# Two more seven-product pairs in a transformer block's down projection, a later place for one pair of residual products, and a later half of the token sums

## The chip, the cores and the metric

The kernel runs on one core of one Trainium2 chip. The time of a kernel is the device time of one execution in microseconds (us), and its figure is the median of several executions. A profile is one further execution, recorded by the hardware profiler: it has a span (from the first to the last recorded work) and a device time of its own, which is a little longer than the span.

Five engines matter. PE (TensorE) multiplies matrices; PEld is its loading of the stationary operand, which overlaps the multiplying. DVE (VectorE) and ACT (ScalarE) work elementwise, POOL (GpSimd) does a few tiny things here, and SP (SyncE) issues the transfers from memory.

## The reference, cut to what matters

One layer of a hybrid encoder with 256 tokens and 2048 features: an input projection, retention and latent attention side by side, an output projection with a normalised residual, and then a feed-forward part:

```
x = LN(alpha * x + concat(A, B) @ W_out)
x = LN(alpha * x + relu(x @ W_up)^2 @ W_down)
```

`W_up` is 2048 x 8192 and `W_down` is 8192 x 2048, all in float32. The change touches only the last product, `relu(...)^2 @ W_down`, and the residual sum behind it.

## The kernel before

**Splitting.** Every float32 operand of a large product is split into a high part `hi` in the narrower format fp32r and the rest, `lo = value - hi`. A product is then three matmuls: `hi*hi`, `hi*lo` and `lo*hi`. ACT makes each `hi` (line 381 for the down projection) and DVE each `lo` (line 382). So each weight that comes from memory passes ACT and DVE once before PE can use it.

**The down projection.** The 8192 rows of `W_down` are 64 blocks of 128, taken two at a time as 32 *pairs*, and the 2048 output columns are two halves, passes `p = 0` and `p = 1`. The tokens are two blocks of 128. In a pass, an ordinary pair takes 24 matmuls of 128x512: 2 row blocks, 2 token blocks, 2 column quarters, 3 split terms (`xstat`, line 297). They accumulate in four PSUM banks `cb`. The `relu^2` values are held in `rr` and split, four row blocks at a time, by `r_split` (lines 969 and 970).

**Seven-product pairs.** A pair is a 2x2 block product (two token blocks, two row blocks, two column quarters), so it can be done with seven block products in place of eight, as in Strassen-Winograd's scheme. Such a pair takes 21 matmuls (line 1062, `seven_products`). For it, DVE and ACT make sums of the tokens (`token_sums`, lines 389 to 395) and sums of the weights (`weight_sums`, lines 401 to 404), and the weights are split in four pieces (three of 1024 columns and one of 512) where an ordinary pair has two of 1024. `SEVEN` (line 38) lists, for each pass, which pairs in order of use are done so: seven in the first, six in the second. The four sums `mb` of such pairs are added to the residual when the last of a pass is done, by `add_sums`.

**Order of the work.** The program order of each engine is written out by hand. The work that prepares weights is a list of jobs, each a list of pieces, and a job's transfer is issued when one of three buffers `raw` comes free (`load_ahead`). The main loop calls `unit()` after each group of matmuls (four times in a pair of either kind). `unit()` first takes each generator in `side` one step further, and then emits up to two pieces, as long as one of the five slots for split weights (`NSLOT`, tile names `hi_wd` and `lo_wd`) is free in program order. In an ordinary pair one `unit()` call stands behind every 6 matmuls.

**The last residual.** In the second pass `add_sums` does one thing more: the residual's last quarter for the second token block, `col(1, 3)`, isn't added by DVE at the end. It is split into `xb` (lines 1035 and 1036) and added into PE's bank `cb[1][1]` by two matmuls with an identity (`identr`, line 1032; the matmuls are line 1040). These matmuls stand 6 steps of the generator, and so 6 `unit()` calls, behind the split. The last four pairs of the second pass (`w_staged`) are kept for the end, where they are used bank by bank so that the normalisation can begin on the first banks.

Of the kernel before, what the change touches and what calls it, by code (L numbers as in the profile page):

```python
# [8 lines left out]
F32 = mybir.dt.float32  # L9
# [25 lines left out]


ORDER = (tuple(range(16)), (14, 15, 11, 12, 13) + tuple(range(11)))
SEVEN = ((2, 6, 10, 14, 18, 22, 26), (2, 6, 10, 14, 18, 22))
KEPT = {11: 0, 12: 1, 13: 2}
NHELD = 4  # L40
STAGE_AT = 24
# [34 lines left out]
def kernel(  # L76
# [19 lines left out]
    nc = tc.nc  # L96
# [60 lines left out]
    def raw_tile(job, name):  # L157
        job.raw = wraw.tile([P, 2048], F32, tag="raw", name=name)
        return job.raw
# [182 lines left out]
    def row_job(i, pieces):  # L342
        def load(job):
            norm_rows[i] = raw_tile(job, f"row{i}")
            nc.sync.dma_start(norm_rows[i], ln_rows[i:i + 1].partition_broadcast(P))
        other(load, pieces)
# [17 lines left out]
    def weights_pair(p, pair, into=None, seven=None):  # L364
        job = Job(None, [], into is None or None in into)

        def load():
            raw = raw_tile(job, f"raw_wd{p}_{pair}")
            nc.sync.dma_start(raw.rearrange("p (e c) -> p e c", e=2),
                              w_down[2 * pair:2 * pair + 2, :, p * 1024:(p + 1) * 1024].rearrange("e p c -> p e c"))  # L370

        def split(i, src, n=1024):
            if into is None or into[i] is None:
                hi = wsp.tile([P, 1024], F32R, tag="hi", name=f"hi_wd{p}_{pair}_{i}")
                lo = wsp.tile([P, 1024], F32R, tag="lo", name=f"lo_wd{p}_{pair}_{i}")
            else:
                o = into[i] * 2048
                hi, lo = extra["sx"][:, o:o + 1024], extra["sx"][:, o + 1024:o + 2048]
            job.hi.append(hi)
            job.lo.append(lo)  # L380
            nc.scalar.copy(hi[:, 0:n], src)  # L381
            nc.vector.tensor_sub(lo[:, 0:n], src, hi[:, 0:n].bitcast(F32))  # L382

        def token_sums():

            k = 2 * pair
            r0, r1 = (rr[k // 32][:, k % 32 + e] for e in range(2))
            st = spare_flat[:, seven * 512:(seven + 1) * 512].rearrange("p (i c) -> p i c", i=4)
            nc.vector.tensor_add(st[:, 0], r0[:, P:], r1[:, P:])
            nc.vector.tensor_sub(st[:, 1], st[:, 0], r0[:, 0:P])  # L390
            nc.vector.tensor_sub(st[:, 2], r0[:, 0:P], r0[:, P:])
            nc.vector.tensor_sub(st[:, 3], r1[:, 0:P], st[:, 1])
            v = sums_of(seven)
            nc.scalar.copy(v[:, :, 0], st)
            nc.vector.tensor_sub(v[:, :, 1], st, v[:, :, 0].bitcast(F32))

        def weight_sums():

            b11, b12, b21, b22 = (job.raw[:, i * 512:(i + 1) * 512] for i in range(4))
            t1, t3, t4 = extra["t13"][:, 0:512], extra["t13"][:, 512:], extra["t4"]  # L400
            nc.vector.tensor_sub(t1, b12, b11)
            nc.vector.tensor_sub(t3, b22, b12)
            nc.vector.tensor_sub(b12, b22, t1)
            nc.vector.tensor_sub(t4, b21, b12)

        job.load = load
        if seven is None:
            job.pieces = [lambda e=e: split(e, job.raw[:, e * 1024:(e + 1) * 1024]) for e in range(2)]
            job.loose = 0 if into is None else 2 - into.count(None)
        else:  # L410
            job.loose = 2
            job.pieces = [token_sums, weight_sums, lambda: split(0, job.raw[:, 1024:]),
                          lambda: split(1, job.raw[:, 0:1024]), lambda: split(2, extra["t13"]),
                          lambda: split(3, extra["t4"], 512)]
        job.free = [[False] for _ in job.pieces[job.loose:]]
        jobs.append(job)
        return job

    def sums_of(q):
        return extra["sx"][:, q * 1024:(q + 1) * 1024].rearrange("p (i h c) -> p i h c", i=4, h=2)  # L420
# [3 lines left out]
    for p in range(2):  # L424
        for n, pair in enumerate(pairs[p]):
            if p == 0 or n < 32 - NHELD:
                j_down[p][pair] = weights_pair(p, pair, None, SEVEN[p].index(n) % 2 if n in SEVEN[p] else None)
                if p == 1 and n == STAGE_AT:
                    pair = pairs[1][32 - NHELD]
                    j_down[1][pair] = weights_pair(1, pair, (2, 3))  # L430
            elif n > 32 - NHELD:
                j_down[p][pair] = weights_pair(p, pair, (1, None) if n == 33 - NHELD else None)
    j_down[0][pairs[0][SEVEN[0][0]]].held = True
    row_job(2, [])
# [528 lines left out]
    def r_split(b, keep=None):  # L963
        if keep is None:
            t = work.tile([P, 4, 512], F32R, tag="big", name="rhl", bufs=2)
        else:
            t = extra["sx"][:, (keep + 1) * 2048:(keep + 2) * 2048].rearrange("p (k t) -> p k t", k=4)
        r = rr[b // 8][:, b % 8 * 4:b % 8 * 4 + 4]
        nc.scalar.copy(t[:, :, 0:S], r)
        nc.vector.tensor_sub(t[:, :, S:], r, t[:, :, 0:S].bitcast(F32))  # L970
        rhls[b] = t
# [28 lines left out]
    extra["t4"] = ut  # L1000
    j_down[0][pairs[0][SEVEN[0][0]]].held = False
    st2 = [stat.tile([P, 4, 6], F32, tag=f"ln{tb}", name=f"lm{tb}", bufs=1) for tb in range(2)]
    u, v = spare_flat[:, 0:512], spare_flat[:, 512:]

    def col(tb, j):
        return xt[:, tb, j * 512:(j + 1) * 512]

    def add_sums(p, mb):

        p1, p6, p5, p7 = mb  # L1010

        def plus(j, tb, src):
            c = col(tb, 2 * p + j)
            nc.vector.scalar_tensor_tensor(c, c, ALPHA, src, op0=ALU.mult, op1=ALU.add)

        nc.scalar.copy(u, p1)
        plus(0, 0, p1)
        yield
        nc.vector.tensor_add(u, u, p6)
        nc.vector.tensor_add(v, u, p7)  # L1020
        yield
        plus(0, 1, v)
        nc.vector.tensor_add(v, v, p5)
        yield
        plus(1, 1, v)
        nc.vector.tensor_add(u, u, p5)
        yield
        plus(1, 0, u)
        if p == 1:

            c = col(1, 3)
            nc.vector.tensor_copy(identr, ident)
            nc.scalar.activation(mask, ident, AF.Copy, scale=-1.0)
            xb = work.tile([P, 2, 512], F32R, tag="xf", name="xb")
            nc.scalar.copy(xb[:, 0], c)
            nc.vector.tensor_sub(xb[:, 1], c, xb[:, 0].bitcast(F32))
            for _ in range(6):
                yield
            for i in range(2):
                nc.tensor.matmul(cb[1][1], identr, xb[:, i], start=False, stop=False)  # L1040
# [7 lines left out]
    def seven_products(p, pair, first, last):  # L1048
        job = j_down[p][pair]
        x, k, q = rhls[pair // 2], pair % 2 * 2, SEVEN[p].index(pairs[p].index(pair)) % 2  # L1050
        for a, w, o, pb, alone in ((("x", 1, 0), 0, 0, cb[0][0], False), (("s", 3), 0, 512, cb[0][1], False),
                                   (("x", 0, 0), 1, 0, mb[0], True), (("s", 1), 1, 512, mb[1], True),
                                   (("s", 0), 2, 0, mb[2], True), (("s", 2), 2, 512, mb[3], True),
                                   (("x", 1, 1), 3, 0, cb[1][0], False)):
            use(job, w + 1)
            if a[0] == "x":
                h, l = (x[:, k + a[1], i * S + a[2] * P:i * S + (a[2] + 1) * P] for i in range(2))
            else:
                h, l = (sums_of(q)[:, a[1], i] for i in range(2))
            hi, lo = job.hi[w][:, o:o + 512], job.lo[w][:, o:o + 512]  # L1060
            for x_part, w_part, fst, lst in ((h, hi, True, False), (h, lo, False, False), (l, hi, False, True)):
                nc.tensor.matmul(pb, x_part, w_part, start=alone and first and fst, stop=alone and last and lst)  # L1062
            if o or w == 3:
                free(job, (w,))
                unit()

    for p in range(2):
        cb = [[(acc, bank)[p](f"d{p}{tb}{j}") for j in range(2)] for tb in range(2)]
        mb = None
        for n, pair in enumerate(pairs[p][:32 if p == 0 else 32 - NHELD]):  # L1070
            b = pair // 2
            if n % 2 == 0:
# [5 lines left out]
                if p == 1 and n == STAGE_AT:  # L1078
                    r_split(ORDER[1][15], -1)
            if n in SEVEN[p]:  # L1080
                if mb is None:
                    mb = [(bank, acc)[p](f"s{p}{j}") for j in range(4)]
                seven_products(p, pair, n == SEVEN[p][0], n == SEVEN[p][-1])
                if n == SEVEN[p][-1]:
                    side.append(add_sums(p, mb))
            else:
                job = j_down[p][pair]
# [152 lines left out]
```

## Time and profile before

| what | value |
|---|---|
| median of 3 runs | 1128.78 us (1127.2 to 1128.94) |
| the profiled execution | 1127.41 us, of which the span is 1125.4 us |
| PE busy | 1115.1 us, 99% of the span |
| DVE busy | 784.4 us, 70% |
| ACT busy | 548.4 us, 49% |
| DMA | 217.14 MB, mean 193 GB/s |
| granted TensorE clock | full (1.00) |
| down projection on PE | from about 773.2 us to 1116.3 us of the span |

A row of the timeline or of the chain of waits has a start in the span, a duration, an engine, a line of the kernel and the tiles that it writes and reads. A row "x4" merges four instructions of one kind; its duration runs from the start of the first to the end of the last. Square brackets give the idle time of the engine in front of the row, and what ended it.

### The profile page before, as it was taken

How to read it: one execution, taken by the hardware profiler on the slowest of the kernel's cores; microseconds unless marked ns; L12 is line 12 of the kernel's file. 1: busy time of each engine (PE TensorE's matmuls, PEld its weight loads, DVE VectorE, ACT ScalarE, POOL GpSimd, SP SyncE). 2: the span in 40 equal slices, each digit the busy share in tenths (PEclk: the TensorE clock that was granted, in tenths of full speed). 3: DMA queues.
4: the chain of work that ended last, by engine and by line, in shares of the span. 5: the costliest groups of instructions: out<-in, count | busy, mean ns of one | idle time of the engine just before them, and what ended most of it. 6: DMA issues, size and time to landing. Idle time of an engine off the chain costs nothing.

```text
span 1125.4 us, 14360 instructions
## 1 busy us (share of the span) xinstructions
PE 1115.1 (99%) x5609; PEld 948.4 (84%) x5609; DVE 784.4 (70%) x1089; ACT 548.4 (49%) x709; POOL 9.6 (1%) x18
## 2 busy tenths in 40 slices
PE   9999999999999999999999999999999999999988
PEld 8888888888888889888888888888888888888875
DVE  6676774656656786555555576657887887887885
ACT  4445564545453555444444444444555554555550
POOL 0000000000000000000000000000000000000000
PEclk9999999999999999999999999999999999999999
DMA  8755374444474635555555565654655555655562
GB/s 292 239 206 178 119 247 158 159 150 164 150 286 173 243 126 190 189 188 191 192 192 191 192 229 190 227 187 151 209 202 187 206 205 186 216 196 187 202 247 75
DMA packets 42387, 217.14 MB, mean 193 GB/s; under 512 B 4176, under 2 KB 5200, under 8 KB 27088
## 3 DMA queue, kind: packets, MB, share of 16 engines
q1 hardware_dynamic: 42176, 215.97, 54.5%
q8 instruction: 44, 0.72, 0.3%
q10 hardware_dynamic: 144, 0.26, 0.1%
q14 instruction: 23, 0.19, 0.0%
HBM read 214.12 MB, written 2.10 MB: 192 GB/s over the span
## 4 chain that ended last, share of the span: by engine, by line
PE 97%; DVE 1%; DMA 1%; issue 0%; ACT 0%; POOL 0%; POOLq 0%; SPq 0%; DVEq 0%
PE d L297 24%; PE up L682 20%; PE r L297 16%; PE up L688 10%; PE o L297 8%; PE m L297 4%; PE s L1062 3%; PE d L1062 2%; PE pu L682 2%; PE pv L297 1%; DMA raw_mla<-in_w_mla 1%; PE pu L688 1%; PE pq L297 1%; PE up L853 1%; PE pms L713 0%; PE pms L712 0%
## 5 line engine op out<-in xcount | busy, mean ns | idle before, releaser
L682 PE MATMUL up<-x1hl,hi_wu 128*128 128x512 f32 x984 | 234.8, 391 | 0.0
L682 PEld LDWEIGHTS up<-x1hl,hi_wu 128*128 128x128 f32 x984 | 180.8, 188 | 35.0
L382 DVE TENSOR_TENSOR lo_wd<-raw_wd,hi_wd 128x1024 fp32r<-128x1024 f32 x125 | 148.9, 1219 | 45.2 <-ACT hi_wd L381 44.6
L186 DVE TENSOR_TENSOR lo_wu<-raw_wu,hi_wu 128x1024 fp32r<-128x1024 f32 x128 | 155.8, 1224 | 22.8 <-ACT hi_wu L185 18.5
L381 ACT CAST hi_wd<-raw_wd 128x1024 fp32r<-128x1024 f32 x125 | 128.9, 1051 | 86.7 <-PE d L297 63.0
L297 PE MATMUL d<-hi_wd,rhl 128*128 128x512 f32 x616 | 167.7, 389 | 0.0
L185 ACT CAST hi_wu<-raw_wu 128x1024 fp32r<-128x1024 f32 x128 | 134.0, 1055 | 30.8 <-PE up L682 26.1
L297 PE MATMUL r<-hi_ret,xhl 128*128 128x512 f32 x512 | 147.1, 397 | 0.0
L297 PEld LDWEIGHTS d<-hi_wd,rhl 128*128 128x128 f32 x616 | 115.6, 188 | 24.0
L688 PEld LDWEIGHTS up<-x1hl,lo_wu 128*128 128x128 f32 x984 | 126.2, 191 | 4.7
L688 PE MATMUL up<-x1hl,lo_wu 128*128 128x256 f32 x984 | 127.7, 283 | 0.0
L297 PEld LDWEIGHTS r<-hi_ret,xhl 128*128 128x128 f32 x512 | 93.9, 188 | 18.2
L957 ACT COPY ut<-up 128x256 f32<-128x256 f32 x64 | 23.8, 372 | 170.0 <-PE up L682 167.4
L958 DVE TENSOR_TENSOR ut<-ut,up 128x256 f32<-128x256 f32 x64 | 26.9, 420 | 106.0 <-ACT ut L957 105.7
L297 PE MATMUL d<-lo_wd,rhl 128*128 128x512 f32 x308 | 95.1, 389 | 0.0
L186 DVE TENSOR_TENSOR lo_ret<-raw_ret,hi_ret 128x1024 fp32r<-128x1024 f32 x64 | 75.7, 1220 | 23.9 <-ACT hi_ret L185 23.7
L297 PE MATMUL r<-lo_ret,xhl 128*128 128x512 f32 x256 | 79.4, 391 | 0.0
L185 ACT CAST hi_ret<-raw_ret 128x1024 fp32r<-128x1024 f32 x64 | 64.9, 1051 | 16.4 <-PE r L297 12.2
L297 PEld LDWEIGHTS d<-lo_wd,rhl 128*128 128x128 f32 x308 | 57.8, 188 | 12.0
L297 PE MATMUL o<-hi_wo,mix 128*128 128x512 f32 x208 | 57.1, 392 | 0.0
L297 PEld LDWEIGHTS r<-lo_ret,xhl 128*128 128x128 f32 x256 | 48.0, 188 | 10.4
L297 PE MATMUL d<-hi_wd,sx 128*128 128x512 f32 x176 | 49.5, 389 | 0.0
(243 smaller groups left out, 1381.3 us busy)
## 6 DMA issues: line engine op xcount, KB each, us to landing
raw_wu<-in_w_up SPq DMA_DIRECT2D x64, 1024.0 KB, 4.8
raw_wd<-in_w_down SPq DMA_DIRECT2D x64, 1024.0 KB, 5.5
raw_ret<-in_w_ret SPq DMA_DIRECT2D x32, 1024.0 KB, 4.8
raw_wo<-in_w_out SPq DMA_DIRECT2D x16, 1024.0 KB, 4.8
raw_mla<-in_w_mla SPq DMA_DIRECT2D x14, 672.0 KB, 5.3
raw_qk<-in_w_qk SPq DMA_DIRECT2D x8, 640.0 KB, 3.9
row<-in_ln_rows SPq DMA_DIRECT2D x4, 1024.0 KB, 5.6
raw_uv<-in_w_uv SPq DMA_DIRECT2D x2, 1024.0 KB, 5.0
```

Of the source, the lines that this page charges most:

```text
L185: nc.scalar.copy(hi[:, o:e], r)
L186: nc.vector.tensor_sub(lo[:, o:e], r, hi[:, o:e].bitcast(F32))
L297: nc.tensor.matmul(accs[j][:, :w], x_part, w_part[:, a:a + w], start=first and fst and i == 0, stop=last and lst and i == len(steps) - 1)
L381: nc.scalar.copy(hi[:, 0:n], src)
L382: nc.vector.tensor_sub(lo[:, 0:n], src, hi[:, 0:n].bitcast(F32))
L682: nc.tensor.matmul(pb, hi[:, a:a + P], hl[:, k0 + i], start=first and i == ks[0], stop=last and i == ks[-1])
L688: nc.tensor.matmul(pb[:, 0:S], lo[:, a:a + P], hl[:, k0 + i, 0:S], start=False, stop=last and i == ks[-1])
L853: nc.tensor.matmul(pb[:, :, t], hi[:, k * P:(k + 1) * P], x1hl[:, k].rearrange("p (a t) -> p a t", a=2)[:, :, t], start=tb == 0 and k == 0 ...
L957: nc.scalar.copy(t, pb[:, S:])
L958: nc.vector.tensor_add(t, t, pb[:, 0:S])
L1062: nc.tensor.matmul(pb, x_part, w_part, start=alone and first and fst, stop=alone and last and lst)
```

## The change

Three edits. The list of seven-product pairs has eight pairs in the first pass and seven in the second (fifteen in all, thirteen before); they stand three or four pairs apart, where they stood four apart. The last DVE instruction of `token_sums`, which makes the low parts of the token sums out of what ACT has just written, is emitted behind the four weight sums in place of ahead of them. And the two matmuls that add the last residual are emitted 12 steps behind its split in place of 6.

```diff
-SEVEN = ((2, 6, 10, 14, 18, 22, 26), (2, 6, 10, 14, 18, 22))
+SEVEN = ((2, 5, 9, 12, 16, 19, 23, 26), (2, 6, 9, 13, 16, 19, 22))
...
             v = sums_of(seven)
             nc.scalar.copy(v[:, :, 0], st)
-            nc.vector.tensor_sub(v[:, :, 1], st, v[:, :, 0].bitcast(F32))
+            job.rest = lambda: nc.vector.tensor_sub(v[:, :, 1], st, v[:, :, 0].bitcast(F32))
...
             nc.vector.tensor_sub(b12, b22, t1)
             nc.vector.tensor_sub(t4, b21, b12)
+            job.rest()
...
             nc.scalar.copy(xb[:, 0], c)
             nc.vector.tensor_sub(xb[:, 1], c, xb[:, 0].bitcast(F32))
-            for _ in range(6):
+            for _ in range(12):
                 yield
             for i in range(2):
                 nc.tensor.matmul(cb[1][1], identr, xb[:, i], start=False, stop=False)
```

## The prediction

> **What bounds the kernel now.** First the page: the span and the busy times.
>
> ```profile
> span 1125.4 us, 14360 instructions
> ...
> PE 1115.1 (99%) x5609; PEld 948.4 (84%) x5609; DVE 784.4 (70%) x1089; ACT 548.4 (49%) x709; POOL 9.6 (1%) x18
> ```
>
> PE is the bound. An edit helps if it takes matmuls away or closes a hole in PE; more work on DVE or ACT costs nothing until it comes late for PE. Next I read what PE and its loads waited for from 770 us to the end, the stretch that the diff touches.
>
> ```profile
> PE d L1040 <- DVE identr L1032: 2.8, 1, 2.8
> PE sh L1154 <- ACT warm L1152: 1.4, 1, 1.4
> ...
> PEld d L1040 <- ACT sx L381: 3.2, 1, 3.2
> ```
>
> Ahead of the final normalisation (L1154) there is one hole in the whole down projection: at the two residual products, L1040. The chain in order of time gives the price of a matmul (four pieces of a regular cycle):
>
> ```profile
> 805.12 1.36 PE d L1062 x6
> 806.48 2.72 PE s L1062 x12
> 809.20 0.68 PE d L1062 x3
> 809.88 16.32 PE d L297 x72
> ```
>
> 72 matmuls in 16.32 us are 0.2267 us each. An ordinary pair (24) takes 5.44 us, a seven-product pair (21) 1.36 + 2.72 + 0.68 = 4.76 us. Four pairs with one of seven take 21.08 us.
>
> **Part 1: two more seven-product pairs.** Each turns 24 matmuls into 21: 3 x 0.2267 = 0.68 us, so 1.36 us for both. That is the whole direct gain; the rest of this part asks whether DVE can pay. Busy time of each engine in one such cycle; the others are alike. Columns: stretch, its length, then PE, PEld, DVE, ACT:
>
> ```profile
> 795.04:816.12 21.08, 21.08 (x95) 17.45 (x94) 17.45 (x21) 12.22 (x14) 0.00 (x0) 1.00 0.57 203
> ```
>
> DVE is busy 17.45 of 21.08 us. What leaves a cycle when it shrinks from four pairs to three is one ordinary pair: two subtractions of 1024 columns, and half of an `r_split` (one per two pairs). Their pace stands in the timeline, four in a row, and their duration and those of the other DVE work in the groups by line and form:
>
> ```profile
> 808.56 4.62 DVE L382 TENSOR_TENSOR lo_wd<-raw_wd,hi_wd 128x1024 fp32r<-128x1024 f32 x4
> ```
>
> ```profile
> L382 DVE TENSOR_TENSOR lo_wd<-raw_wd,hi_wd 128x1024 fp32r<-128x1024 f32 x121 | 144.0, 1219 | 44.4 <-ACT hi_wd L381 44.0
> ...
> L970 DVE TENSOR_TENSOR rhl<-rr,rhl 128x1024 fp32r<-128x1024 f32 x22 | 26.8, 1218 | 0.1
> ...
> L395 DVE TENSOR_TENSOR sx<-xm,sx 128x512 fp32r<-128x512 f32 x13 | 9.0, 692 | 8.9 <-ACT sx L394 8.9
> ...
> L390 DVE TENSOR_TENSOR xm<-xm,rr 128x128 f32<-128x128 f32 x13 | 3.8, 292 | 0.5
> ```
>
> In a run each starts (4.62 - 1.22)/3 = 1.13 us behind the one ahead, so the pair that goes is worth 2.5 x 1.13 = 2.83 us of DVE. A three-pair cycle therefore needs 17.45 - 2.83 = 14.6 us of DVE, and PE takes 2 x 5.44 + 4.76 = 15.64 us for it: DVE at 93%, 1.0 us to spare. The new lists have four three-pair gaps in the first pass (2-5, 9-12, 16-19, 23-26) and four in the second (6-9, 13-16, 16-19, 19-22); only the last three stand in a row. The spare time has to hold DVE's waits too: the groups show 8.9/13 = 0.69 us per seven-product pair on ACT's copy of the token sums, and 44.4 us on `hi_wd`. ACT in turn waited for PE to free a slot, so DVE was early there:
>
> ```profile
> ACT hi_wd L381 <- PE d L297: 88.8, 60, 3.1
> ```
>
> ACT has 12.2 of 21.08 us and no trouble. DVE is in time, so I cost its side at nothing. What covers it is PE's 15.64 us; if DVE took more, each us above would cost PE up to 8 us in all.
>
> [...] By whole durations a three-pair cycle would be 4 x 0.29 for the token sums, 6 x 0.69 for the six instructions of 512 columns and 3 x 1.22 for the three of 1024 (8.96 us in the seven-product pair), plus 5.5 x 1.22 (6.71 us) for the rest: 15.67 us against PE's 15.64, no slack, though hardly a loss. [...]
>
> **Part 2: the later half of the token sums.** No instruction is added or removed. ACT's copy of the sums now runs while DVE does the four weight sums (2.8 us), which need nothing of it, so the 0.69 us wait of each seven-product pair goes: 15 x 0.69 = 10 us of DVE. PE did not wait there, so this is worth 0.0 us by itself; it widens part 1's spare time. What moves back is the low part of the sums, by these four subtractions; PE first reads it in a pair's second product, behind pieces that DVE makes later still. Nothing is late.
>
> **Part 3: the residual products six steps later.** The hole, with the DVE queue that made it:
>
> ```profile
> 1068.98 1.05 ACT L381 CAST hi_wd<-raw_wd 128x1024 fp32r<-128x1024 f32 x1 [3.15 <-PE d L297]
> ...
> 1070.06 1.23 DVE L382 TENSOR_TENSOR lo_wd<-raw_wd,hi_wd 128x1024 fp32r<-128x1024 f32 x1 [2.10 <-ACT hi_wd L381]
> ...
> 1077.86 0.61 PE L297 MATMUL d<-hi_wd,rhl 128*128 128x512 f32 x2
> ...
> 1080.31 0.68 DVE L1014 SCALAR_TENSOR_TENSOR xm<-xm 128x512 f32<-128x512 f32 x1
> 1080.91 0.22 DVE L1032 CAST identr<-ident 128x128 fp32r<-128x128 f32 x1
> 1081.05 0.68 DVE L1036 TENSOR_TENSOR xb<-xm,xb 128x512 fp32r<-128x512 f32 x1
> 1081.27 1.00 PE L1040 MATMUL d<-xb,identr 128*128 128x512 f32 x2 [2.80 <-DVE identr L1032]
> 1081.65 2.35 DVE L382 TENSOR_TENSOR lo_wd<-raw_wd,hi_wd 128x1024 fp32r<-128x1024 f32 x2
> ...
> 1082.11 0.62 PE L297 MATMUL d<-hi_wd,rhl 128*128 128x512 f32 x2
> ```
>
> The two matmuls that start at 1077.86 and 0.23 later are the last ones; without a wait the products would start at 1078.32 and 1078.54 and the next ordinary matmul at 1078.77. It started at 1082.11: **3.34 us lost**. Moved by six `unit()` calls of 6 matmuls, the products stand 36 x 0.2267 = 8.16 us further on, at 1086.48, and `xb` is done at 1081.05 + 0.68 = 1081.73: 4.75 us early. They stay ahead of the staged pairs (5 + 12 = 17 of the 20 calls left).
>
> What is late next? DVE runs from 1070.06 without a break, and the first item behind `xb` is the second half of pair 26, ready at 1081.65 + 1.22 = 1082.87. PE, no longer held, has six matmuls of pair 25 and twelve of pair 26's first half ahead of it (18 x 0.2267 = 4.08 us behind 1078.32, so 1082.40) and reads that low part with the third matmul, 1082.85. It is met to within 0.02 us. The subtraction behind it is due 2.72 us later and ready 1.13 us later: 1.6 us to spare. I take 0.05 us, and 0 to 1 us as bounds, since any delay here shows one for one. The start of DVE's run is ACT's copy at 1068.98. Its row names PE, but a load that DVE's progress released fits as well:
>
> ```profile
> raw_wd<-in_w_down SPq DMA_DIRECT2D x64, 1024.0 KB, 5.5
> ```
>
> One issued 5.5 us ahead, at about 1063.4, would land just there. Either way the start keeps its distance from PE when all that is ahead moves. Behind it, the staged pairs (from the DVE timeline and ACT's):
>
> ```profile
> 1094.55 1.05 ACT L381 CAST hi_wd<-raw_wd 128x1024 fp32r<-128x1024 f32 x1 [1.67 <-PE d L297]
> ...
> 1095.64 1.22 DVE L382 TENSOR_TENSOR lo_wd<-raw_wd,hi_wd 128x1024 fp32r<-128x1024 f32 x1 [1.49 <-ACT hi_wd L381]
> ...
> 1102.71 0.69 DVE L764 TENSOR_TENSOR xm<-xm,d 128x512 f32<-128x512 f32 x1 [5.25 <-PE d L297]
> ```
>
> The last weight piece was ready at 1096.86 because ACT waited for PE. PE begins the staged pairs 3.3 us earlier, at 1082.11 + 54 x 0.2267 - 3.3 = 1091.05, and reads that piece 34 matmuls on, at 1098.8: even unmoved it is in time by 1.9 us. DVE then waits 5.25 us for PE, so PE still sets the end, and the tail behind it is the same.
>
> **The sum**, against the profiled execution: 1127.41 - 1.36 - 0 - 3.34 + 0.05 = 1122.8 us. The shown runs go from 1127.2 to 1128.94 with the profiled one near their lower end; the mean of these four executions is 1128.08, and less 4.65 that is 1123.4. I say **1123.5 us**, with 1122 to 1125 as this case's own range.
>
> **The rivals.**
>
> *The hole moves (1125.5 to 1126.7).* Loads that land a us or more later, or DVE later by as much, hold PE at pair 26 in place of L1040. For it: the 0.02 us above. Against it: the queue is the same as before and only PE's demand comes earlier, so little more than the slip itself is lost. If 2 of the 3.34 us stay, the gain is 2.65 us (1125.5); if all stay, 1.36 us (1126.7).
>
> *DVE becomes the bound (slower).* Place: the eight three-pair cycles, where a cycle that takes DVE longer than 15.64 us holds PE for the difference. It eats the gain of 4.65 us at 15.64 + 4.65/8 = 16.2 us and makes the kernel slower by over 0.2% from 16.5 us. At 16.7 us it costs 8.5 us: 1127.41 + 3.8, about 1131 us, or 1132 as a median. For it: 1.0 us to spare out of 15.6 by the pace. Against it: 1.9 us are missing to the point where it decides, and part 2 takes a wait away.
>
> *The edit of the list is lost in part.* If seven of the eight three-pair cycles run 0.2 us over, 1.4 us go and part 3 alone is left: 1128.08 - 3.3, about 1125.
>
> **How the numbers follow.** This kernel's measurement can tell about 0.2%, 2.26 us, from no change, so faster means below 1126.5 us against the median. Forecast 0.78, all faster. The hole moves: 0.13, of which 0.05 is still faster. List lost in part: 0.05, of which 0.02 is for more lost than that and falls within 0.2%. DVE bound: 0.04, slower. That makes 0.86 faster, 0.10 the same, 0.04 slower. The range of 8 in 10 takes the forecast's own spread and the bounds of the moved hole: 1122 to 1126.5.
>
> **What would show it.** Right: 72 matmuls still in 16.32 us, pieces of 4.76 us fifteen times, no PE wait at L1040, a wait below 1 us at `lo_wd` of pair 26 or none, and L395 without idle time ahead of it. Wrong: PE waits on `lo_wd` L382 inside the three-pair cycles (DVE bound), or a new PE wait above 1 us past 1070 us.

## The result, and the profile after

| | before | after |
|---|---|---|
| median | 1128.86 us (4 runs, 1127.2 to 1129.07) | 1122.59 us (4 runs, 1121.6 to 1122.91) |
| profiled execution | 1127.41 us, span 1125.4 us | 1121.6 us, span 1119.8 us |

The ratio is 0.9946, with a 95% interval of 0.9931 to 0.9962: 6.3 us faster by the medians (the interval says 4.3 to 7.8 us), 5.8 us by the two profiled executions. The forecast was 4.65 us, to 1123.5 us.

The page of the changed kernel, and what PE and its loads waited for from 765 us to the end:

```profile
span 1119.8 us, 14377 instructions
...
PE 1112.9 (99%) x5603; PEld 947.1 (85%) x5603; DVE 796.4 (71%) x1111; ACT 552.9 (49%) x715; POOL 9.6 (1%) x18
```

```profile
PE sh L1155 <- ACT warm L1153: 1.4, 1, 1.4
...
PEld d L297 <- DVE lo_wd L382: 0.2, 1, 0.2
```

The wait at the residual products (line 1041 in the changed kernel) is gone, and one of 0.2 us on a weight's low part is new. The chain of waits, in order of time, runs through PE from the first matmul of the down projection to the last. Its start, a three-pair cycle, and its end:

```profile
772.13 10.88 PE d L297 x48
...
1040.73 1.36 PE d L1063 x6
1042.09 2.72 PE s L1063 x12
1044.81 0.68 PE d L1063 x3
1045.49 10.88 PE d L297 x48
...
1061.13 23.24 PE d L297 x102
1084.37 0.45 PE d L1041 x2
1084.83 25.85 PE d L297 x114
1110.68 0.02 issue
```

A seven-product pair still takes 4.76 us, and 48 matmuls 10.88 us (0.2267 each). The two residual products take 0.45 us, without waiting. From 772.13 to 1110.68 the down projection takes 338.55 us, where it took 343.13 us before (773.16 to 1116.29). So of the 5.6 us between the two spans, **4.58 us lie where the change is**, and 1.03 us lie ahead of it, in code that both kernels share. The chains of the first 60 us show where: in the profiled execution of before, a first weight load came later.

```profile
4.92 6.45 DMA raw_mla<-in_w_mla
...
13.76 46.32 PE m L297 x229
```

```profile
12.39 47.78 PE m L297 x238
```

These are before and after. That 1 us is a difference between executions, not an effect of the change: in a second profile of the changed kernel (`after_again`, below) the down projection starts at 772.98 us, near the 773.16 us of before, and takes 338.52 us. But the medians differ by more than 4.58 us too, and the experiments had to say why.

How DVE fares in the three-pair cycles (columns: stretch, its length, PE, PEld, DVE, ACT; after):

```profile
1014.21:1029.85 15.64, 15.64 (x71) 12.95 (x70) 14.36 (x20) 10.00 (x12) 0.00 (x0) 1.00 0.58 202
1029.85:1045.49 15.64, 15.64 (x71) 12.95 (x70) 14.77 (x19) 9.38 (x11) 0.00 (x0) 1.00 0.59 202
1045.49:1061.13 15.64, 15.64 (x71) 12.95 (x70) 14.36 (x20) 10.00 (x12) 0.00 (x0) 1.00 0.58 202
```

DVE is busy 14.4 to 14.8 of 15.64 us (14.6 was forecast), and PE is never held. Its wait ahead of the low token sums is gone, as the group by line shows (it was 8.9 us in 13):

```profile
L395 DVE TENSOR_TENSOR sx<-xm,sx 128x512 fp32r<-128x512 f32 x15 | 10.3, 684 | 0.0
```

And the place that was said to be met to within 0.02 us, pair 26's second half (timeline of PEld and of ACT):

```profile
1080.45 0.30 PEld L297 LDWEIGHTS d<-lo_wd,rhl 128*128 128x128 f32 x2 [0.25 <-DVE lo_wd L382]
```

```profile
1066.50 1.05 ACT L381 CAST hi_wd<-raw_wd 128x1024 fp32r<-128x1024 f32 x1 [3.06 <-DMA raw_wd<-in_w_down]
```

PE's load waits 0.25 us there, and the copy that starts DVE's run is released by a transfer, the reading that the row of before left open. SyncE issued that transfer at 1061.07 us here and at 1063.45 us in the profile of before, where the prediction took 1063.4.

### The profile page after: what moved, and what is told of

Same layout as the page of the kernel before. It is cut to its first block, busy times and chain, and to the rows that moved or that the text cites. A ratio compares the mean times of both kernels' runs of the same rounds, so it can differ in the third digit from the quotient of the medians.

```text
span 1119.8 us, 14377 instructions
## 1 busy us (share of the span) xinstructions
PE 1112.9 (99%) x5603; PEld 947.1 (85%) x5603; DVE 796.4 (71%) x1111; ACT 552.9 (49%) x715; POOL 9.6 (1%) x18
## 4 chain that ended last, share of the span: by engine, by line
PE 99%; DVE 1%; POOL 0%; issue 0%; POOLq 0%; ACT 0%; DVEq 0%
PE d L297 24%; PE up L683 20%; PE r L297 16%; PE up L689 11%; PE o L297 8%; PE m L297 5%; PE s L1063 4%; PE d L1063 3%; PE pu L683 2%; PE pv L297 1%; PE pu L689 1%; PE pq L297 1%; PE m L461 1%; PE up L854 1%; PE pms L714 0%; PE pms L713 0%
## 5 line engine op out<-in xcount | busy, mean ns | idle before, releaser
L297 PE MATMUL d<-hi_wd,rhl 128*128 128x512 f32 x600 | 163.8, 389 | 0.0
L297 PEld LDWEIGHTS d<-hi_wd,rhl 128*128 128x128 f32 x600 | 112.6, 188 | 23.4
L297 PE MATMUL d<-lo_wd,rhl 128*128 128x512 f32 x300 | 92.8, 389 | 0.0
L297 PE MATMUL d<-hi_wd,sx 128*128 128x512 f32 x160 | 45.4, 389 | 0.0
```

Of the source, the lines that this page charges most:

```text
L297: nc.tensor.matmul(accs[j][:, :w], x_part, w_part[:, a:a + w], start=first and fst and i == 0, stop=last and lst and i == len(steps) - 1)
```

## The experiments

Times "before" in this section are medians of further runs of the kernel before on the same chip as the experiment: 1128.61 us for the first four, 1128.80 us for the next four, 1128.68 us for the last. The changed kernel's 1122.87 us, to which the later kernels are compared, was measured beside the first four; the later ones ran on two other chips, on which before's medians differ from the first by 0.2 us at most.

### Each part alone, and the whole again

**The residual products alone.**

```diff
-            for _ in range(6):
+            for _ in range(12):
                 yield
```

> Before, with the residual products 12 steps behind their split in place of 6; the list and the token sums as before. Theory (the hole of 3.34 us in front of the products is all that this part is worth, and PE is next held by the low part of pair 26, by 0.2 us or so): 3.1 us faster than before, PE without a wait at L1040 and a wait of 0.1 to 0.4 us on lo_wd. Rival (the products only trade their wait for one at the staged pairs): less than 1.5 us faster, with a new wait past 1085 us. A second rival: this part brings 4.5 us or more, because the earlier PE also pulls work forward that held the end; then the tail behind the last matmul (9.1 us of span) is shorter.

Measured: 1124.12 us, ratio 0.9963 (0.995 to 0.9975): 4.5 us faster by the medians. PE's loads waited 0.3 us on `lo_wd`, and nothing waited at the products. By size that is the second rival's 4.5 us, not the theory's 3.1 us. But the tail is not shorter: its two groups of matmuls (L1146 and L1154) start 3.24 us apart as before (1113.09 and 1116.33, where they were 1116.11 and 1119.35). So the rival's mechanism falls. In the profiled execution the down projection takes 339.95 us (773.32 to 1113.27), 3.18 us less than in that of before, which is the theory's size. So 1.3 us more, in the medians alone, wanted a cause.

**The list alone.**

```diff
-SEVEN = ((2, 6, 10, 14, 18, 22, 26), (2, 6, 10, 14, 18, 22))
+SEVEN = ((2, 5, 9, 12, 16, 19, 23, 26), (2, 6, 9, 13, 16, 19, 22))
```

> Before, with the list of fifteen pairs; the low token sums and the residual products where they were. Theory (a matmul not issued is 0.2267 us, and DVE has 1.0 us to spare in a three-pair cycle, of which its wait for ACT takes 0.69): 1.36 us faster than before, L395 still with 0.69 us idle ahead of each, no PE wait but the 2.8 us at L1040. Rival (DVE has no room without the moved low sums): waits of PE on lo_wd or sx in the three-pair cycles, 0 to 1.4 us lost, no gain.

Measured: 1127.11 us, ratio 0.9987 (0.9979 to 0.9996), 1.5 us faster. DVE still waited 10.3 us in 15 pairs ahead of L395 (0.69 each), and PE waited for nothing but the 2.7 us at L1040. The theory holds, and the three-pair cycles would also have been carried without the moved token sums.

**The token sums alone** (the list and the 6 steps of before).

> Before, with only the low token sums behind the weight sums. Theory (DVE time off the path): DVE's 0.69 us wait ahead of L395 is gone in all 13, the time is the same as before within 0.3 us. Rival (DVE's hand-overs reach PE somewhere that the trace does not name): 1 us or more faster.

Measured: 1128.71 us, ratio 1.0003 (0.9994 to 1.0012). DVE's wait is gone, and the time is the same.

**The changed kernel again.**

> The changed kernel once more, beside the runs of before on this chip. Theory (the parts add up: 1.36 + 3.34 less 0.2): 4.5 us faster, and the 6.3 us between the first medians was partly the spread of the runs. Rival (the change brings 6 us or more, something beyond the counted terms): 6 us faster with an interval that leaves 4.5 out; then the first 770 us of the span must be shorter too.

Measured: 1122.87 us, ratio 0.9952 (0.9939 to 0.9966), 5.7 us faster. It is between the two expectations, and the interval holds both (3.8 to 6.9 us). The first 770 us are not shorter, as the rival wanted: the down projection starts at 772.98 us. The three parts alone add up to 4.5 + 1.5 - 0.1 = 5.9 us, so within the noise the parts are additive, and the surplus is in the residual products.

### What the hole cost beyond its length

Two of these profiles show it. The token sums alone keep the hole; the granted clock behind it (the column ahead of the last two) and PE's timeline are these:

```profile
1080.00:1084.00 4.00, 2.65 (x6) 2.07 (x7) 4.00 (x7) 1.10 (x2) 0.00 (x0) 0.66 0.02 2
1084.00:1088.00 4.00, 4.00 (x17) 3.25 (x17) 4.00 (x5) 2.00 (x2) 0.00 (x0) 0.92 0.91 302
```

```profile
1081.35 1.30 PE L1041 MATMUL d<-xb,identr 128*128 128x512 f32 x2 [2.69 <-DVE identr L1033]
1082.44 1.06 PE L297 MATMUL d<-hi_wd,rhl 128*128 128x512 f32 x2
1083.30 1.06 PE L297 MATMUL d<-lo_wd,rhl 128*128 128x512 f32 x2
1084.15 1.33 PE L297 MATMUL d<-hi_wd,rhl 128*128 128x512 f32 x4
1085.32 0.62 PE L297 MATMUL d<-lo_wd,rhl 128*128 128x512 f32 x2
```

After 2.69 us without a matmul the granted clock was 0.66 in the next 4 us. Eight matmuls took from 1082.44 to 1085.32, 2.88 us in place of 1.81, and the two products 1.09 us in place of the 0.84 us that they took in the profile of before: 1.3 us lost. The list alone shows the same (0.63 behind a hole of 2.66 us). The profiled execution of before did not: its hole of 2.80 us was followed by a clock of 1.00. The mean granted clock is on record for every run, not for the profiled ones alone, and it splits the times. Of the 21 runs of before beside these four kernels, the seven with a mean of 0.999 or 1.000 took 1126.46 to 1127.81 us, and the fourteen with 0.997 or 0.998 took 1127.92 to 1129.36 us; their medians, 1127.16 and 1128.74 us, lie 1.6 us apart. All ten runs of the two kernels without the hole, the residual products alone and the changed kernel, have 0.999 or 1.000. Against the seven runs whose clock held, the residual products alone gain 3.0 us, which is the theory's size, and the changed kernel 4.3 us. A mean does not say where in a run the clock fell; that it was behind the hole is what the two profiles show. Two kernels change the hole's length alone, by one step of six matmuls each.

```diff
-            for _ in range(6):
+            for _ in range(7):
```

> Before, with the residual products 7 steps behind their split in place of 6: the hole ahead of them shrinks by six matmuls, 1.36 us, to an idle time of about 1.4 us. Theory (a hole of 2.7 to 2.8 us idle makes the granted clock drop for some 3 us afterwards in a part of the executions, at a price of 1.3 us; a hole of 1.4 us does not): 2.0 to 2.4 us faster than before by the medians, runs within 1.2 us of each other, granted clock 1.00 behind the hole. Rival (the hole costs its length and the two clusters of before's times come from elsewhere): 1.36 us faster, and runs spread over 2.5 us as before's are.

Measured: 1126.11 us, ratio 0.9975 (0.9965 to 0.9985), 2.7 us faster; the hole was 1.2 us idle, and the clock behind it 1.00. Eight of the nine runs have a mean clock of 0.999 or 1.000; the ninth, the longest, is listed with 0.949, which nothing here explains. The runs lie within 1.6 us, not 1.2.

```diff
-            for _ in range(6):
+            for _ in range(5):
```

> Before, with the residual products 5 steps behind their split in place of 6: the hole grows by 1.36 us to an idle time of about 4.1 us. Theory (the clock drops behind it in all or nearly all executions): 1.8 to 2.2 us slower than before by the medians, granted clock below 0.8 in the 4 us behind the hole, runs within 1.2 us of each other. Rival (length alone): 1.36 us slower, spread as before.

Measured: 1130.62 us, ratio 1.0019 (1.0011 to 1.0028), 1.8 us slower; the hole was 4.0 us idle. The windows behind it:

```profile
1080.00:1084.00 4.00, 2.32 (x5) 1.78 (x6) 4.00 (x6) 1.23 (x2) 0.00 (x0) 0.62 0.00 0
1084.00:1088.00 4.00, 4.00 (x11) 3.10 (x10) 2.67 (x3) 0.00 (x0) 0.00 (x0) 0.52 0.83 287
```

With a shorter hole the gain is 2.7 us. Length alone gives 1.36 us by the step and 1.6 us by the idle times (2.8 to 1.2), and the interval of 1.7 to 4.0 us leaves out both, the second only just. With a longer one the loss is 1.8 us; length alone, 1.36 us, is within that interval (1.2 to 3.2 us), but the clock fell for twice as long in the profile, and all eleven runs have a mean clock of 0.996 to 0.998, where three of the 19 runs of before on that chip have 1.000. The spread of its runs, 2.6 us, is not what the theory expected; the four runs with 0.998 took 1129.86 to 1130.52 us and the seven with 0.996 or 0.997 took 1130.22 to 1132.41 us, so the drop differs in size from run to run. Taken together, by the mean clocks: a drop shows in a part of the executions with a hole of 2.7 to 2.8 us (0.997 or 0.998 in 14 of the 21 runs of before), in all eleven with one of 4.0 us (0.996 to 0.998), and in none of the ten runs of the two kernels that close it (0.999 or 1.000). The two groups of before's times match these cases run by run. Whether the length decides is not settled here (one of the kernels below adds to it).

### How near DVE is to being the bound

Three kernels make the low token sums several times over, with the same values, three, five and seven times, and so add DVE work to each seven-product pair and nothing else. The first:

```diff
-            job.rest()
+            for _ in range(3):
+                job.rest()
```

> The changed kernel with the low token sums made three times over in place of once (the same values): 2 x 0.60 = 1.2 us more DVE in each seven-product pair, 15.8 us in a three-pair stretch against PE's 15.64. Theory (1.0 us to spare in each three-pair stretch): the spare time is just used up, 0 to 1 us slower than the changed kernel. Rival (there is no spare time; every us of DVE is handed on to PE): 15 x 1.2, well over 5 us slower.

Measured: 1124.71 us, 1.8 us above the changed kernel's 1122.87. In its profile the down projection takes 339.80 us, 1.3 us more than the changed kernel's 338.52. No wait stands at a three-pair gap: PE's loads wait 0.6 us at the first seven-product pair of the second pass and 1.0 us at pair 26 near the end (0.2 us in the changed kernel).

> The same with five times over: 2.4 us more DVE in each seven-product pair, 17.0 us in a three-pair stretch, 1.4 us over PE's time, while a four-pair stretch (20.0 of 21.08 us) pays 1.1 us back. Theory: waits of PE of some tenths to 2 us at the end of most three-pair stretches, 4 to 8 us slower than the changed kernel in all. Rival (DVE has far more room than its busy time shows): under 1.5 us slower.

Measured: 1134.50 us, 11.6 us above.

> The same with seven times over: 3.6 us more DVE in each seven-product pair, 18.2 us in a three-pair stretch, 2.6 us over, and a four-pair stretch (21.2 us) pays nothing back. Theory: each further us shows in full at eight three-pair gaps, 8 x 2.6 = 20.8 us less the lead at the start, 18 to 25 us slower than the changed kernel. Rival (DVE has far more room): under 5 us slower.

Measured: 1157.28 us, 34.4 us above. All three cost more than the theory said, the last by 9 us or more. The timeline of the last has the main reason, and one of PE's waits:

```profile
861.90 4.33 DVE L395 TENSOR_TENSOR sx<-xm,sx 128x512 fp32r<-128x512 f32 x6
```

```profile
844.20 0.79 PE L1064 MATMUL d<-lo_wd,rhl 128*128 128x512 f32 x1 [2.12 <-DVE lo_wd L382]
```

Instructions that write the same tile one after another stood (4.33 - 0.69)/5 = 0.73 us apart, not 0.60. With 0.73 the three-pair cycle needs 14.6 + 1.46 = 16.1, 17.5 and 19.0 us, and the four-pair cycle 17.6 + 1.46 = 19.1, 20.5 and 22.0 us, against PE's 15.64 and 21.08. Counted so afterwards, four more cost 8 x 1.9 - 5 x 0.6 = 12 us (11.6 measured). Six more cost 8 x 3.4 + 5 x 0.9 = 32 us (34.4 measured); the rest may be the clock, which was 0.50 behind the wait shown, from 845 to 850 us, and 0.993 over the whole span. For two more, 8 x 0.5 us is less than what the four-pair cycles pay back (5 x 2.0), and the waits seen are indeed elsewhere. PE's waits of the middle kernel:

```profile
PE d L1064 <- DVE lo_wd L382: 2.9, 4, 1.0
PE s L1064 <- DVE lo_wd L382: 1.6, 1, 1.6
```

So the limit is near where the busy times put it: up to 1.0 us more DVE in a three-pair cycle is free by the count, 1.46 us more was still carried, by the count because four-pair cycles stand between, and with 2.92 us more PE pays what the count says.

**Every second pair.**

```diff
-SEVEN = ((2, 5, 9, 12, 16, 19, 23, 26), (2, 6, 9, 13, 16, 19, 22))
+SEVEN = (tuple(range(2, 27, 2)), tuple(range(2, 23, 2)))
```

> The changed kernel with every second pair done with seven products, 24 in all. A two-pair stretch is 10.2 us of PE and, by the same count as for three, 14.6 - 2.8 = 11.8 us of DVE. Theory (DVE's busy time per stretch sets the bound): DVE without a break inside the passes, PE held 1.3 to 1.6 us in each of the 22 two-pair stretches, 27 to 34 us in all; the nine further pairs save 6.1 us of matmuls, so 21 to 28 us slower than the changed kernel, 1144 to 1151 us. Rival (the limit is only in the slots and hand-overs, and DVE can go faster when PE waits): under 10 us slower.

Measured: 1143.83 us, 21.0 us above the changed kernel and 1.3% slower than before (1.0116 to 1.0149). The largest of PE's waits:

```profile
PE d L1063 <- DVE lo_wd L382: 19.6, 18, 1.1
```

These are 18 waits of 1.1 us each. The loads behind them waited longer:

```profile
PEld d L1063 <- DVE lo_wd L382: 27.6, 19, 1.5
```

That is 1.5 us each, within the 1.3 to 1.6 expected, and 27.6 us in all is what the time asks for: 21.0 us lost and 6.1 us of matmuls saved. Here 24 pairs save more matmuls and lose.

### Versions beyond the change

```diff
-SEVEN = ((2, 5, 9, 12, 16, 19, 23, 26), (2, 6, 9, 13, 16, 19, 22))
+SEVEN = ((2, 5, 8, 11, 14, 17, 20, 23, 26), (2, 5, 8, 11, 14, 16, 19, 22))
```

> The changed kernel with seventeen seven-product pairs, nearly all three pairs apart, once two (14 to 16). Theory (0.68 us a pair as long as DVE keeps 93% in a three-pair stretch, however many stand in a row): 1.36 us below the changed kernel, about 1121.5 us, no PE wait on lo_wd but the 0.2 us near the end. Rival (the four-pair gaps were what let DVE catch up): waits of PE on lo_wd from the third or fourth three-pair gap on, 0.5 us or more each, and a time at or above the changed kernel's 1122.9 us.

Measured: 1121.93 us, ratio to before 0.9937 (0.9924 to 0.9949), 0.9 us below the changed kernel, where 1.36 were expected; its runs spread over 2.2 us, so the medians alone do not show this gain. In the profile the down projection takes 337.96 us, 0.6 us less than the changed kernel's. No wait stands in the cycles. Near the end, at pair 26, PE waited longer than in the changed kernel (timeline of all engines):

```profile
1066.86 1.05 ACT L381 CAST hi_wd<-raw_wd 128x1024 fp32r<-128x1024 f32 x1 [3.84 <-DMA raw_wd<-in_w_down]
...
1080.80 0.73 PE L297 MATMUL d<-lo_wd,rhl 128*128 128x512 f32 x2 [0.60 <-DVE lo_wd L382]
```

The transfer of pair 25 kept ACT waiting 0.8 us longer than in the changed kernel, and PE's wait for the low part became 0.6 us (1.0 us for its load). This is the first rival of the prediction, in small.

```diff
-SEVEN = ((2, 5, 9, 12, 16, 19, 23, 26), (2, 6, 9, 13, 16, 19, 22))
+SEVEN = ((2, 5, 7, 10, 12, 15, 18, 21, 23, 26), (2, 5, 8, 11, 14, 16, 19, 22))
```

> The changed kernel with eighteen seven-product pairs; the first pass has two pairs in place of three between some (2 5 7 10 12 15 18 21 23 26). A two-pair stretch needs 14.6 - 2.8 = 11.8 us of DVE against 10.2 us of PE, so it borrows 1.6 us from what DVE is ahead. Theory (a single two-pair stretch is carried by DVE's lead of 2 to 3 us, and the three-pair one behind it pays 1.0 us back): 2.0 us below the changed kernel, about 1120.9 us, perhaps with waits of some tenths in the first pass. Rival (no lead to borrow from): 1.6 us lost at each of the three two-pair stretches, 1125 us or more.

Measured: 1120.77 us (1120.61 to 1120.99), ratio to before 0.9926 (0.9914 to 0.9939), 2.1 us below the changed kernel, as expected. The only wait in the passes is again one of PE's loads, 0.2 us at `lo_wd`. It is the fastest kernel of this study. Each of its four two-pair stretches is followed by a three-pair one, and no wait stands there; with every second pair, where none is, nearly each costs 1.5 us. That DVE's lead pays for them fits, but the lead itself was not measured.

## Why the prediction was right

**The sum.** 1.36 + 3.34 - 0.05 = 4.65 us was forecast for the down projection; the profiled executions differ by 4.58 us there, and the second profile of the changed kernel by 4.61. The direction held, and the range did with 0.6 us to spare: the median was 0.9 us below the forecast.

**Part 1, the list.** 0.68 us a pair, 1.36 us in all: 1.5 us measured alone (0.5 to 2.4). That DVE has 1.0 us to spare in a three-pair cycle held (14.4 to 14.8 of 15.64 us busy), and of the runs with more DVE work the first, at 16.1 us by the count, was still carried at the three-pair gaps, the second, at 17.5, was not. The longer count by whole durations (15.67 us) is not what DVE showed: four subtractions in a row took 4.62 us, where four times 1.22 are 4.88, its cycles are shorter than 15.67 us and PE does not wait.

**Part 2, the token sums.** Nothing by itself (1.0003), as forecast. The further claim that it widens the spare time holds in the profile, but the list alone shows that it was not needed.

**Part 3, the residual products.** The hole is closed, its length was right, and what was late next was named to the pair: 0.25 us at pair 26 where 0.05 us was taken. Too small was the price of the hole for the medians. The sum took the 3.34 us of one execution, in which the granted clock stayed at 1.00 behind the hole, and left out that in others it falls and costs more: 1.3 us in a profile, 1.6 us between the medians of the two groups. Since 14 of the 21 runs of before were of that kind (mean clock 0.997 or 0.998), the median gains most of that as well: 4.3 us against the runs whose clock held, near the 4.65 forecast, and 5.7 us against all. The term that was mis-sized is this one: 3.34 us taken, 4.5 us measured with that part alone (2.8 to 5.6). That the range took it in is in part luck, since nothing in it was meant for the clock.

**The rivals.** The hole that moves was right as a mechanism (a late transfer shows one for one at pair 26: with seventeen pairs ACT's copy started 0.36 us later than in the changed kernel, 1066.86 for 1066.50, and PE's load 0.35 us later, 1080.80 for 1080.45), at 0.2 to 0.6 us in place of 2 to 3 us. DVE as the bound is real, but its price was put too high (the gain gone at 16.2 us, slower from 16.5): with 16.1 us of DVE in a three-pair cycle the kernel lost 1.8 us of its gain where 8 x 0.46 = 3.7 us were due, and with 17.5 us it lost 11.6 us where 14.9 were due. The prediction left out that four-pair cycles pay back. At 17.5 us it was slower than before (ratio 1.0054, 1.0039 to 1.0069). The change stays below it. The list lost in part did not happen.

## What to carry to other kernels

Count the off-path engine's busy time per cycle of the schedule, not as a share of the kernel: 71% over the span was 93% in the cycles that changed, 1 us from the bound, and work could be packed closer still (18 pairs, 1120.77 us) where looser cycles stood between the tight ones; with every second pair it took 1143.83 us. When a hole is closed, look for what is due next with the same care; here it was met to within a few tenths of a us (a load waited 0.25 us at pair 26), and a transfer's landing then set the rest. A hole in the matmul stream cost more than its length here (1.3 us more behind one of 2.69 us), so a sum from one profiled execution should ask whether the clock stayed up behind it, and the mean granted clock of every other run tells how often it did.

## What the hardware showed that was not expected

The granted clock fell to 0.66 and 0.63 in the windows from 1080 to 1084 us that hold the end of holes of 2.69 and 2.66 us, to 0.62 and then 0.52 at one of 4.0 us, and not at all behind a hole of 2.80 us in another execution or one of 1.2 us. In the kernel with six more of the low token sums it was 0.50 from 845 to 850 us, behind a wait of PE of 2.12 us, and 0.90 in the next 5 us. So no single length separates the cases: it fell behind 2.12 us in one execution and stayed up behind 2.80 us in another. Why like holes lowered it at one time and not at another, no run here shows.

The other surprise is DVE's pace: instructions of 512 columns stood 0.73 us apart where each wrote the tile of the one ahead, and 0.60 us apart where they were independent (in the profile of the changed kernel the two at L401 and L402 start at 1032.88 and 1033.48 us). By the count above, that moved the largest of these runs by some 11 us, from 20.8 to 32.
